# A two-layer MLP on one core: where the sums of the first two passes stand in VectorE's order

## The chip, the cores and the metric

The kernel runs on one core of a Trainium2 chip. The metric is the device time of one execution in microseconds (us), as the median of several executions of the same program. Lower is better.

## The reference

```python
def setup_inputs():
    batch, seq_len, hidden_dim = 8, 1024, 1024
    intermediate_dim = 4 * hidden_dim
    # x (8, 1024, 1024), w1 (1024, 4096), w2 (4096, 1024), all float32

def reference(x, w1, w2):
    h = x @ w1
    h = 0.5 * h * (1 + np.tanh(np.sqrt(2 / np.pi) * (h + 0.044715 * h ** 3)))
    return (h @ w2).astype(np.float32)
```

Two matrix products with a tanh GELU between them: 8192 rows of x, 1024 to 4096 to 1024 columns.

## The kernel before

**Passes.** The 8192 rows are worked in eight passes of 1024 rows (`sb` 0 to 7). A pass is `matmul1` (x times w1, GELU, result g in SBUF) and then a second product (g times w2, rows of the output). The operands are float16, the sums in PSUM and in the `tmp` tiles float32.

**Seven products instead of eight.** Each matrix is cut into 2 x 2 blocks, "11", "12", "21", "22", and the block product is made from seven products of sums of blocks (the Winograd form of Strassen's method). The sums of w are `W_SUM`: sum 5 is 12 - 11, sum 6 is 22 - sum 5, sum 7 is 22 - 12, sum 4 is 21 - sum 6. The sums of x (or g) are `S_SUM`; in `XOps.make` sum 7 is written over block 21. Products 1, 2 and 3 take raw blocks of w. From the third pass on some products are split a second time in the same way; the operands for that ("inner" sums) are made during the first two passes and stored in DRAM.

**The first pass** loads w1 and w2 in float32, casts them and writes the raw float16 blocks to DRAM (`raw_d`, `raw2_d`). **The second pass** (`sb == 1`) reads w1 back in four "quads" of four column chunks (`MadeQuad`): four loads per quad on the SP queue, one per block, then the sums 5, 6, 7, 4 on VectorE, each stored to `w1_d` on the POOL queue, and inner sums (`inner_sums(2)` and `inner_sums(3)`, four small sums each, one store each). Passes three to eight read all of that back ready made and are alike.

**The first m2** is `matmul2_made` with `sb == 0`. Its seven products come in the order 1, 2, 5, 6, 3, 7, 4, each of four row quarters q of 16 matmuls. After a quarter, `post(m, q, bank)` moves the bank out: for products 2, 3 and 7 VectorE adds the bank to a `tmp` tile, for products 1, 5, 6 and 4 ScalarE copies it. Products 6, 7 and 4 go on accumulating in the banks of product 1, so quarter q of product 4 can start only after VectorE has read that bank in `post(7, q)`. After `post`, `run((m, q))` issues the jobs of the table `FILL[0]`: "x5" is sum 5 of the next pass's x, "q5" sum 5 of the first quad of w1, "i2" its inner sums of product 2. The quad's loads are issued at (3, 3); those of the next x are 16 transposing DMAs on the SP queue, issued at (6, 3).

**matmul1 of the second pass** runs over eight pairs j of column chunks. Pair 0 has 12 products of four matmuls, each later pair 14, in the order 1, 1, 4, 4 (of the pair before), 2, 2, 5, 5, 6, 6, 3, 3, 7, 7. VectorE adds the result of product 2 to the tile of product 1 (`add(a[h], banks_b[h])`), then makes `difference(j - 1)`; later it adds product 7 (`add(p5[h], banks_a[h])`) and product 3 (`add(t[h], banks_c[h])`). Product 4 accumulates in the same bank as 1, 6 and 7, so it needs the read of product 7's add. Between these stand the jobs of the pair:

- `ahead(j)`: in an even pair the sums 5 and 6 of the next quad, in an odd pair its sums 7 and 4 and the inner sums 2 and 3;
- `splits`: four sums of a half of a w2 block for the inner level, from `split_in_m1`, for pairs 1 to 4. They work in `gc` tiles, of which there are four: two that a load fills and two for results. The next set's loads wait for the sums that read the tiles before, its sums for the stores (POOL queue, `in_d`) that read the result tiles before.

The first half of the list is issued after `difference`, the rest at the end of the pair. `steady(j)` issues, in four of the pairs, two DMAs each on the POOL queue that cast 256 rows of the x of the third pass to float16 in DRAM (`xb`), each behind a small POOL copy (`pace`) that waits for a GELU.

**Order.** Each engine works through its instructions in order. Matmuls, the VectorE sums with `pin`, copies and GELUs keep the order of the program (`keep_in_program_order`); the other loads and stores are placed by the scheduler.

Of the kernel before, what the change touches and what calls it, by code (L numbers as in the profile page):

```python
# [22 lines left out]
BLOCKS = ("11", "21", "12", "22")  # L23
# [3 lines left out]
SPLIT_IN_M1 = (2, 3)  # L27


def slots(table):  # L30
    return {(int(k[0]), int(k[1])): v.split() for k, v in (row.split(":") for row in table.split(";"))}
# [4 lines left out]
    ;20:g50 w50 w51;21:g51 w52;22:w53 g52;23:g53  # L36
    ;50:w60 w61;51:w62 w63;52:g30 g31;53:g32 g33
    ;60:w70 w71;61:w72 w73;62:w40 w41;63:w42 w43
    ;30:x5;31:x7;32:x6;33:x3
    ;70:q5;71:q6;72:q7;73:q4  # L40
    ;40:i2;41:i3""".replace("\n    ", "")),
    slots("""10:g60 w50;11:g61 w51;12:g62 w52;13:g63 w53
    ;20:g50 p55;21:g51 p56;22:g52 p57;23:g53 p54
    ;50:w60 w61;51:w62 w63;52:g30 g31;53:g32 g33
# [18 lines left out]
def kernel(  # L63
# [7 lines left out]
    nc = tc.nc  # L71
# [33 lines left out]
    raw_d = [dram.tile([P, 4, KH * QW], DT, name=f"raw_d{q}") for q in range(NI // QC)]  # L105
# [4 lines left out]
    def psum():  # L110
        return pp.tile([P, HT], F32, name="ps")

    def temp():
        return tp.tile([P, HT], F32, name="tmp")

    def unit(rows, cols):
        return up.tile([P, rows, cols], DT, name="u")

    def tt(out, in0, in1, op, pin=False):
        i = nc.vector.tensor_tensor(out=out, in0=in0, in1=in1, op=op)  # L120
        if pin:
            tc.keep_in_program_order(i)
# [4 lines left out]
    def flat(t):  # L127
        return t.rearrange("p a b -> p (a b)")
# [31 lines left out]
    class MadeQuad:  # L160


        def __init__(self, q, first, store):
            self.q, self.first, self.store = q, first, store
            self.raw = {b: unit(2 * KH, 2 * P) for b in BLOCKS}
            self.ops = {m: self.raw[b] for m, b in W_TERM.items()}
            if not first:
                for b, t in self.raw.items():
                    nc.sync.dma_start(out=flat(t), in_=raw_d[q][:, BLOCKS.index(b), :])

        def load(self):

# [66 lines left out]
    def stored(d, raw, m):  # L239
        return raw[:, BLOCKS.index(W_TERM[m]), :] if m in W_TERM else d[:, SUMS.index(m), :]  # L240
# [56 lines left out]
    def x_blocks():  # L297
        return {b: unit(KH, HT) for b in ("22", "21", "12", "11")}
# [75 lines left out]
    def x_cast_paced(s, g_chunk, q, xb):  # L374

        mark = nc.gpsimd.tensor_copy(out=pace, in_=g_chunk[:, :2])  # L376
        return x_cast(s, mark, range(q * P, (q + 2) * P, P), xb)

    def x_transpose(xb, dma, blocks=None, which=range(4)):
        blocks = blocks or x_blocks()  # L380
        for b, t in [list(blocks.items())[i] for i in which]:
            a, k = int(b[0]) - 1, int(b[1]) - 1
            for j in range(KH):
                dma(
                    t[:, j, :],
                    xb[a * HT:(a + 1) * HT, (k * KH + j) * P:(k * KH + j + 1) * P],
                    transpose=True,
                )
        return blocks
# [3 lines left out]
    def matmul1(xs, sb, quads, start=None):  # L393
# [69 lines left out]
        def ahead(j):  # L463

            if sb > 1 or j // 2 == NI // QC - 1:
                return ()
            q, second = divmod(j, 2)
            if not second:
                quad = MadeQuad(q + 1, sb == 0, sb == 1)
                quads.append(quad)  # L470
                if sb == 0:
                    quad.load()
                    quads[q].keep_raw()
            quad = quads[q + 1]
            if sb == 0:
                return [lambda m=m: quad.sum(m, pin=True) for m in SUMS] if second else ()
            jobs = [lambda m=m: quad.sum(m, pin=True) for m in ((7, 4) if second else (5, 6))]
            if sb == 1:
                if second:
                    jobs += [lambda m=m: quad.inner_sums(m) for m in INNER_1]  # L480
            return jobs

        def steady(j):

            if 0 < sb < NSB - 1:
                when = (0, 1, 2, 3) if sb > 1 else (0, 1, 5, 6)
                if j in when:
                    nxt["xb"] = x_cast_paced(sb + 1, g["11"][:, 2 * j + 1, :], 2 * when.index(j), nxt.get("xb"))
                if j == 3 and sb > 1:
                    nxt["blocks"] = x_blocks()  # L490
                if j > 3 and sb > 1:
                    x_transpose(nxt["xb"], load_in_order, nxt["blocks"], range(j - 4, j - 3))
            if sb > 1 and j == 5:
                early[7] = gcp.tile([P, NI // 2, HT // 2], GT, name="gc")
                u, v = (inner_block(g["22"], b) for b in ("11", "21"))
                nc.gpsimd.tensor_tensor(out=early[7], in0=u, in1=v, op=SUB)  # L496

        nxt, early = {}, {}
        splits = []
        late = None  # L500
        pending = []
        for j in range(NI // 2):
# [5 lines left out]
            else:  # L508
                source = quads[j // 2]
            jobs = [] if start is not None and j == 0 else list(ahead(j))  # L510
            if sb == 1:
                jobs += splits
                splits = []
            banks_a = [psum(), psum()]
            a = [temp(), temp()]
            for h in range(2):
# [2 lines left out]
            banks_c, p5, t = [], [], [temp(), temp()]  # L519
# [32 lines left out]
            if start is not None and j == 0:  # L552
                start.more()
                quads[0].load_cols(1, 2, 2, nc.gpsimd.tensor_copy)()
                jobs = list(ahead(j))
            half = (len(jobs) + 1) // 2
            for job in jobs[:half]:
                job()
            def six(h):
# [59 lines left out]
                late = (source, cs, banks_a, t)  # L619
            for job in jobs[half:]:  # L620
                job()
            if start is not None and j == 0:
                for m in SUMS:
                    quads[0].sum(m, (2, 2), True)
            if sb == 1 and j < 2 * len(SPLIT_IN_M1):
                m, h = SPLIT_IN_M1[j // 2], j % 2
                splits = split_in_m1(m, h)
            steady(j)
        difference(NI // 2 - 1)
        blocks = nxt.get("blocks")  # L630
# [160 lines left out]
    def split_in_m1(m, h):  # L791

        raw, t = [], {}
        for k in range(2):
            raw.append(gcp.tile([P, 2, HALF], DT, name="gc"))
            q = 2 * k + h
            nc.sync.dma_start(out=flat(raw[k]), in_=stored(w2_d[q], raw2_d[q], m))

        def make(i, n):
            u, op, v = W_SUM[n]  # L800
            if i % 2 == 0:
                t["two"] = gcp.tile([P, 2, HALF], DT, name="gc")
            t[n] = t["two"][:, i % 2]
            in0, in1 = (
                t[b] if isinstance(b, int) else raw[int(b[0]) - 1][:, int(b[1]) - 1] for b in (u, v)
            )
            tt(t[n], in0, in1, op, True)
            nc.gpsimd.dma_start(  # L808
                out=in_d[m][:, i, h * QC:(h + 1) * QC, :].rearrange("p c n -> p (c n)"), in_=t[n]
            )  # L810

        return [lambda i=i, n=n: make(i, n) for i, n in enumerate(SUMS)]

    def inner_block(t, b):
        a, k = int(b[0]) - 1, int(b[1]) - 1
        return t[:, k * NI // 2:(k + 1) * NI // 2, a * HT // 2:(a + 1) * HT // 2]
# [171 lines left out]
    for sb in range(NSB):  # L988
        g, early, nxt = matmul1(xs, sb, quads, first if sb == 0 else None)
        if sb < 2:  # L990
            xs, quads = matmul2_made(sb, g, None if sb else quads[-1].keep_raw, nxt)
            continue
        matmul2(sb, g, early, nxt)
        if nxt is not None:
            xs, quads = nxt, [StoredHalf(0)]
# [30 lines left out]
```

## Time and profile before

| | |
|---|---|
| time, median of 6 runs | 1502.23 us (1497.42 to 1503.43) |
| the profiled execution | 1501.29 us, span 1499.5 us, mean granted TensorE clock 0.998 |
| TensorE busy | 1477.8 us (99% of the span) |
| VectorE busy | 1157.7 us (77%) |
| ScalarE busy | 615.6 us (41%) |
| GpSimd busy | 234.0 us (16%) |
| DMA | 453.70 MB, mean 303 GB/s |
| the pieces of the first two passes | first m2 from 116.9 to 217.0 us, matmul1 of the second pass from 217.0 to 318.6 us, its m2 to about 416 us |

The profile names tiles without buffer numbers: `u` are the tiles of weights and of x, `gc` the staging tiles, `tmp` the float32 tiles, `ps` the PSUM banks, `raw_d` stands for both raw weights in DRAM, `w_d` for the stored sums, `in_d` for the stored inner operands. L399 are the matmuls of matmul1, L900 those of the made m2, L859 those of the inner level; L120 is the helper behind every VectorE sum, L136 the ScalarE copy, L133 a load in order. A bracket behind a row of the timeline is the idle time before it and what ended it. Times in a row are from the span's start.

### The profile page before, as it was taken

What the parts mean: (1) busy time and instruction counts of PE and PEld (TensorE: products, weight loads), DVE (VectorE), ACT (ScalarE), POOL (GpSimd) and SP (SyncE); (2) the same over time, 40 slices, a digit from 0 to 9 for tenths busy, and PEclk for the clock granted to TensorE, in tenths of its full rate; (3) what the DMA queues carried; (4) which work ended last, traced back from release to release, by engine and by line L of the source; (5) the groups of instructions that cost most, each with busy time, mean ns of one, the idle gap of its engine ahead of it and who ended that gap; (6) DMA issues with size and microseconds to landing.
All of it is one profiled execution on the core that took longest, in us unless ns stands there. A gap on an engine that the chain in (4) does not pass through costs nothing.

```text
span 1499.5 us, 26271 instructions
## 1 busy us (share of the span) xinstructions
PE 1477.8 (99%) x9839; PEld 959.5 (64%) x9839; DVE 1157.7 (77%) x1796; ACT 615.6 (41%) x1157; POOL 234.0 (16%) x315
## 2 busy tenths in 40 slices
PE   7999999999999999999999999999999999999998
PEld 3444444444455688557875588755886568855687
DVE  6756548747767799768997799877997779877787
ACT  5665116541056511664126631366214662156510
POOL 3552023202301011010121000110011101101011
PEclk9999999999999999999999999999999999999999
DMA  9999998977898899999999999998999989997896
GB/s 325 340 347 386 256 332 273 395 220 252 316 324 196 307 297 309 342 241 358 295 312 334 220 381 311 302 320 234 360 302 319 292 266 348 295 366 242 296 283 207
DMA packets 242719, 453.70 MB, mean 303 GB/s; under 512 B 80672, under 2 KB 85792, under 8 KB 241696
## 3 DMA queue, kind: packets, MB, share of 16 engines
q1 hardware_dynamic: 215680, 358.69, 71.3%
q0 software_dynamic: 26912, 93.34, 21.1%
q8 instruction: 77, 1.26, 0.3%
q14 instruction: 50, 0.41, 0.1%
HBM read 355.47 MB, written 111.15 MB: 311 GB/s over the span
## 4 chain that ended last, share of the span: by engine, by line
PE 85%; DMA 5%; issue 4%; DVE 3%; SPq 1%; POOL 1%; ACT 1%; POOLq 0%; DVEq 0%; ACTq 0%
PE ps L399 44%; PE ps L859 34%; PE ps L900 7%; DMA u<-in_w_dram 2%; DVE u L120 1%; DVE tmp L120 1%; SPq L133 1%; DMA in_d<-gc 1%; DMA u<-raw_d 1%; DMA u<-in_x_dram 1%; DMA out_dram<-tmp 1%; DMA xb<-in_x_dram 1%; POOL in_d L808 0%; ACT u L136 0%; POOL w_d L214 0%
## 5 line engine op out<-in xcount | busy, mean ns | idle before, releaser
L399 PE MATMUL ps<-u 128*128 128x512 f16 (+1 forms) x4160 | 762.5, 345 | 10.7 <-DVE tmp L120 5.0
L399 PEld LDWEIGHTS <-u 128*128 128x128 f16 x4160 | 407.0, 98 | 363.2 <-issue 19.3
L120 DVE TENSOR_TENSOR tmp<-tmp,ps 128x256 f32<-128x256 f32 (+1 forms) x936 | 453.7, 532 | 238.3 <-PE ps L399 160.9
L136 ACT COPY tmp<-ps 128x512 f32<-128x512 f32 x416 | 234.8, 581 | 303.3 <-PE ps L399 156.9
L412 ACT ACTIVATE g<-tmp 128x512 f16<-128x512 f32 x384 | 241.8, 633 | 174.6 <-DVE tmp L120 174.5
L859 PE MATMUL ps<-u,gc 128*128 128x256 f16 x2688 | 300.4, 273 | 0.0
L859 PEld LDWEIGHTS <-gc 128*128 128x128 f16 x2688 | 262.5, 98 | 31.1
L120 DVE TENSOR_TENSOR u<-u 128x2048 f16<-128x2048 f16 (+3 forms) x296 | 228.3, 810 | 44.2 <-DMA u<-xb 14.8
L859 PE MATMUL ps<-u,g 128*128 128x256 f16 x2016 | 227.9, 273 | 0.0
L136 ACT COPY u<-ps 128x512 f32<-128x512 f32 (+1 forms) x136 | 78.7, 587 | 346.0 <-PE ps L859 341.4
L859 PEld LDWEIGHTS <-g 128*128 128x128 f16 x2016 | 197.2, 98 | 24.1
L650 POOL DMA_DIRECT2D out_dram<-u x70 | 64.0, 988 | 710.2 <-issue 365.8
L120 DVE TENSOR_TENSOR u<-u,ps 128x512 f32<-128x512 f32 x216 | 147.5, 683 | 34.7 <-PE ps L859 28.9
L900 PE MATMUL ps<-u,g 128*128 128x512 f16 x768 | 166.6, 379 | 3.1 <-DVE tmp L120 3.1
L900 PEld LDWEIGHTS <-g 128*128 128x128 f16 x768 | 75.2, 98 | 93.8 <-issue 3.3
L120 DVE TENSOR_TENSOR g<-g,g 128x2048 f16<-128x2048 f16 (+1 forms) x136 | 131.1, 985 | 1.6 <-ACT g L412 1.6
L120 DVE TENSOR_TENSOR gc<-g,gc 128x2048 f16<-128x2048 f16 x84 | 102.3, 1218 | 0.6
L120 DVE TENSOR_TENSOR gc<-g 128x2048 f16<-128x2048 f16 x78 | 94.9, 1217 | 0.0
L412 ACT ACTIVATE g<-ps 128x512 f16<-128x512 f32 x128 | 76.5, 598 | 10.2 <-PE ps L399 6.9
L139 POOL CAST u<-gc 128x1024 f16<-128x1024 f32 x40 | 47.9, 1206 | 39.5 <-DMA gc<-in_w_dram 32.8
L496 POOL TENSOR_TENSOR gc<-g 128x2048 f16<-128x2048 f16 x6 | 24.4, 4064 | 61.6 <-ACT g L412 61.6
L376 POOL COPY pace<-g 128x2 f16<-128x2 f16 x24 | 4.4, 184 | 185.3 <-ACT g L412 185.3
(32 smaller groups left out, 225.9 us busy)
## 6 DMA issues: line engine op xcount, KB each, us to landing
u<-w_d SPq DMA_DIRECT2D x336, 256.0 KB, 6.3
u<-in_d SPq DMA_DIRECT2D x168, 512.0 KB, 6.8
u<-raw_d SPq DMA_DIRECT2D x252, 256.0 KB, 7.1
out_dram<-u POOLq DMA_DIRECT2D x70, 512.0 KB, 9.2
gc<-in_w_dram SPq DMA_DIRECT2D x48, 512.0 KB, 5.8
u<-in_d SPq DMA_DIRECT2D x96, 256.0 KB, 7.5
raw_d<-u SPq DMA_DIRECT2D x32, 512.0 KB, 9.5
u<-raw_d SPq DMA_DIRECT2D x32, 512.0 KB, 9.0
```

The source lines that it names most:

```text
L120: i = nc.vector.tensor_tensor(out=out, in0=in0, in1=in1, op=op)
L133: return tc.keep_in_program_order(nc.sync.dma_start(out=out, in_=in_, **kw))
L136: tc.keep_in_program_order(nc.scalar.copy(out=out, in_=in_))
L139: pool_last[0] = nc.gpsimd.tensor_copy(out=out, in_=in_)
L376: mark = nc.gpsimd.tensor_copy(out=pace, in_=g_chunk[:, :2])
L399: tc.keep_in_program_order(nc.tensor.matmul(bank, lhsT=w, rhs=x, start=first and k == 0, stop=k == n - 1, skip_group_check=not first,))
L412: gelu_last[0] = nc.scalar.activation(out=g[b][:, c, :], in_=src, func=GELU)
L496: nc.gpsimd.tensor_tensor(out=early[7], in0=u, in1=v, op=SUB)
L650: return nc.gpsimd.dma_start(out=rows, in_=src, **kw)
L859: tc.keep_in_program_order(nc.tensor.matmul(bank[:, i * OH // 2:(i + 1) * OH // 2], lhsT=t[:, c, i * P:(i + 1) * P], rhs=self.y[j][:, c, : ...
L900: tc.keep_in_program_order(nc.tensor.matmul(pair(bank), lhsT=a[:, c, :], rhs=chunks(pieces[c // QC])[:, :, c % QC, :], start=(first and c ...
```

## The change

Four edits. In `FILL[0]` the sums of the next x move from product 3 (and those of the quad from product 7) to the end: x5 after (7, 0), x7 after (7, 3), then x6, x3, the quad's sums and the inner sums during product 4. `MadeQuad` loads its blocks in the order 12, 11, 22, 21 instead of 11, 21, 12, 22. In matmul1 of the second pass an even pair issues all its jobs at its end, an odd pair the first three (sum 7, sum 4, inner sums 2) after `difference` and the fourth at its end; the splits always come last in a pair. The casts of x for the third pass are issued in pairs 4, 5, 6, 7 instead of 0, 1, 5, 6.

```diff
@@ FILL[0]
-    ;30:x5;31:x7;32:x6;33:x3
-    ;70:q5;71:q6;72:q7;73:q4
-    ;40:i2;41:i3""".replace("\n    ", "")),
+    ;70:x5;73:x7;40:x6 x3;41:q5 q6;42:q7 q4
+    ;43:i2 i3""".replace("\n    ", "")),
@@ MadeQuad
             if not first:
-                for b, t in self.raw.items():
-                    nc.sync.dma_start(out=flat(t), in_=raw_d[q][:, BLOCKS.index(b), :])
+                for b in ("12", "11", "22", "21"):
+                    nc.sync.dma_start(out=flat(self.raw[b]), in_=raw_d[q][:, BLOCKS.index(b), :])
@@ steady
-                when = (0, 1, 2, 3) if sb > 1 else (0, 1, 5, 6)
+                when = (0, 1, 2, 3) if sb > 1 else (4, 5, 6, 7)
@@ matmul1, the loop over pairs
             jobs = [] if start is not None and j == 0 else list(ahead(j))
-            if sb == 1:
-                jobs += splits
-                splits = []
...
             half = (len(jobs) + 1) // 2
+            if sb == 1:
+                half = 3 if j % 2 else 0
+                jobs += splits
+                splits = []
             for job in jobs[:half]:
                 job()
...
             for job in jobs[half:]:
                 job()
+            if sb == 1 and j < 2 * len(SPLIT_IN_M1):
+                splits = split_in_m1(SPLIT_IN_M1[j // 2], j % 2)
             if start is not None and j == 0:
                 for m in SUMS:
                     quads[0].sum(m, (2, 2), True)
-            if sb == 1 and j < 2 * len(SPLIT_IN_M1):
-                m, h = SPLIT_IN_M1[j // 2], j % 2
-                splits = split_in_m1(m, h)
             steady(j)
```

## The prediction

> **What bounds the kernel now.** I read the page first: TensorE is busy 99% of the span and the chain that ended last is 85% TensorE. So a change can only give back TensorE's idle time, or add to it. Where that idle time lies is told by TensorE's timeline from 110 to 330 us, where first the made m2 (L900) and then matmul1 of the second pass (L399) run.
>
> ```profile
> PE 1477.8 (99%) x9839; PEld 959.5 (64%) x9839; DVE 1157.7 (77%) x1796; ACT 615.6 (41%) x1157; POOL 234.0 (16%) x315
> ```
> ```profile
> 116.87 41.60 PE L900 MATMUL ps<-u,g 128*128 128x512 f16 x192
> ...
> 206.62 10.52 PE L900 MATMUL ps<-u,g 128*128 128x512 f16 x48 [3.05 <-DVE tmp L120]
> 216.97 36.42 PE L399 MATMUL ps<-u 128*128 128x512 f16 x168
> 253.60 24.33 PE L399 MATMUL ps<-u 128*128 128x512 f16 x112 [0.20 <-DVE tmp L120]
> 281.00 37.80 PE L399 MATMUL ps<-u 128*128 128x512 f16 x168 [3.07 <-DVE tmp L120]
> ```
>
> The reader is to see three holes, 3.05, 0.20 and 3.07 us, each ended by a VectorE add out of a bank, and that the last 168 matmuls take 37.80 us where the first 168 take 36.42. In the chain of waits the later passes run on almost without a hole, so what these two passes gain or lose reaches the end undiminished. Why VectorE was late stands in its own timeline (rows of VectorE alone):
>
> ```profile
> 204.74 1.23 DVE L120 TENSOR_TENSOR u<-u 128x2048 f16<-128x2048 f16 x1 [6.10 <-DMA u<-raw_d]
> 205.88 0.68 DVE L120 TENSOR_TENSOR tmp<-tmp,ps 128x512 f32<-128x512 f32 x1
> ...
> 252.25 0.69 DVE L120 TENSOR_TENSOR gc<-gc 128x1024 f16<-128x1024 f16 x1 [3.70 <-DMA gc<-raw_d]
> ...
> 279.66 0.69 DVE L120 TENSOR_TENSOR gc<-gc 128x1024 f16<-128x1024 f16 x1 [3.60 <-DMA in_d<-gc]
> 280.27 2.47 DVE L120 TENSOR_TENSOR tmp<-tmp,ps 128x512 f32<-128x512 f32 x4
> ```
>
> At 204.74 the sum q5 had waited 6.10 us for the quad's load, and the add behind it (`post(7, 1)`) held up product 4. At 252.25 and 279.66 the first split sum stood in the middle of an even pair (2 and 4) and waited for its load, or for the store of the result tile it overwrites; the adds of product 7 queued behind it. The chain says how long that store took: 11.42 us from issue.
>
> **The change part by part.** Nothing is computed anew: the same sums, loads and stores stand in another order. The working is on the clock of the profile before.
>
> *First m2.* Before (7, 1) VectorE now has only x5. It needs the first eight transposes of x; before, the same sum began at 181.78 after waiting for them, and (7, 0) ends at 172.3 + 14.0 (product 3) + 3.5 = 189.8. So x5 no longer waits and the four adds of product 7 follow TensorE by under 1 us. Then come x7, x6, x3, q5, q6, q7, q4 (1.14 us each in a row: seven make 8.0) and eight small sums (0.37 each, 3.0): from 200.7 to 211.7 if the data are there. x7 needs the last transposes, done by 193.35. q5 comes at 204.1 and needs blocks 12 and 11, now the first two loads on SP (192) ahead of the two `gc` loads that preceded them; before, the third of the quad landed at 204.6, behind those two. Product 4 needs no VectorE sum after (7, 3): ScalarE empties its banks. Matmul1 then starts at 200.1 + 13.9 = 214.0 and wants q5 and x5 2.6 us later. On POOL the four stores of quad sums now stand among those of product 4, 0.54 us each, while its tiles are wanted again only in pair 1, over 10 us on. Saved: 3.05 us, and 0.1 us for the 48 matmuls behind the hole (0.219 against 0.217 each). Cost: nothing, covered by 2 us of VectorE slack at 211.7.
>
> *Splits to the end of a pair.* A pair takes 14 x 4 x 0.2168 = 12.1 us. Each set now has a pair between its loads or stores and the next set, where before the sets of pairs 1 and 2, and 3 and 4, were about half a pair apart. The holes of 0.20 and 3.07 us go.
>
> The clock belongs to the last. Windows of 1 us around it:
>
> ```profile
> 278.00:281.00 3.00, 0.00 (x1) 0.90 1.02 396
> 281.00:282.00 1.00, 1.00 (x3) 0.50 1.01 414
> 282.00:283.00 1.00, 1.00 (x4) 0.50 1.05 430
> 283.00:284.00 1.00, 1.00 (x4) 0.59 1.02 418
> 284.00:285.00 1.00, 1.00 (x7) 1.00 1.01 414
> ```
>
> The columns are TensorE's busy time, its granted clock, the DMA share and GB/s. After the hole the clock is halved for some 2.8 us; 37.80 - 36.42 = 1.38 us are lost by it. The Trainium skill (TensorE: Matmul & The Clock Gate, "The HAM clock gate") says that the gate halves the clock after an idle window of about 3.4 us, windows running free. By that rule a hole of 3.07 us costs only itself, and the gain is 3.05 + 0.20 + 3.07 = 6.3. The trace has two such holes: after 206.6 the clock stayed at 1.00, after 281.0 it fell to 0.50. The trace decides: 6.3 + 0.1 + 1.4 = 7.8 us to be had.
>
> *What the new order asks of VectorE.* Pair 2 ends at 251.6; its last add is done at 253.6, then q5, q6 (2.3) and four splits (0.64 each, 2.6) run to 258.5. Pair 3's adds of product 2 could start at 256.8, so they are 1.7 us late; two adds, `difference`, q7, q4 and four small sums (1.2 + 0.6 + 2.3 + 1.5) end at 264.0, the first add of product 7 at 264.6. Product 4 wants it at 263.8 + 1.73 = 265.5. Slack 0.9 us; pair 5 has the same. ScalarE's GELUs of pairs 3 and 5 come as much later, and its copies behind them still beat product 7 by about 1 us. So a VectorE wait at the end of pair 2 or 4 costs TensorE what it exceeds 0.9 us by.
>
> *The wait that could come.* The sets at the ends of pairs 3 and 4 are the critical ones. The second store of the older set is issued near 269.2, and the newer set starts at 280.2. Stores issued there before took:
>
> ```profile
> in_d<-gc POOLq DMA_DIRECT2D x4, 256.0 KB, 11.8
> ```
>
> (DMA issues from 266 to 272 us: number, size, median us to landing.) With the chain's 11.42 us it lands at 280.6: a wait of 0.4, cost nothing. With 12.9, the longest that the in_d rows show, the wait is 1.9 and the cost 1.0. The `gc` load of that set took 9.5 us and is issued near 270.5: about even. I take 0.5 us, near the low end because the row is of the same transfer in the same stretch.
>
> *The casts.* Two pairs' casts leave 226 to 241 us and enter near 275 (pair 4) and 310 (pair 7): per pair 1 MB read and 0.5 MB written. From 264 to 306 the DMA share is already about 1.0 at some 420 GB/s, so pair 4's cast can push others back by at most 1.5 / 0.42 = 3.6 us. The store above is issued 6 us earlier, so I give it none of that; the upper end is 12.9 + 3.6 = 16.5 us to landing, a wait of 5.5, a hole of 4.6 and a half-clock spell of 1.4: 6.0. The lower end is nothing: TensorE has no further idle time to win. Pair 7's cast lands near 320, 60 us before its first sum. On POOL a cast waits for its GELU ahead of w_d stores of q5 and q6, which are not yet made then.
>
> *Loads in the order 12, 11, 22, 21.* In the built order block 21 of the third and fourth quad falls behind the split loads on SP, which wait for VectorE; sum 4 wants it about a pair later. Nothing.
>
> *Sum.* 7.8 - 0.5 = 7.3 us. Profiled execution: 1501.29 - 7.3 = 1494.0. That run is 0.9 us under the median; from the median, 1502.23 - 7.3 = **1494.9 us**.
>
> **The rivals.**
> 1. *Half of it.* The split's wait moves to the end of pair 4 with a cost near that of before (3 us and the clock, 4.4), and only the first m2 gains: 1502.2 - 3.4 = 1498.8 us. For: 11.8 us to landing against 11.0 us of time. Against: the slack of 0.9 us, and fewer casts in flight before 245 us.
> 2. *Slower.* The late casts clog the saturated stretch. The place is the set at the end of pair 4, the price each us that its older stores land later than 11.9 us after issue (11.0 of distance plus 0.9 of slack), plus 1.4 for the clock. With 7.8 regained it decides at 11.9 + 7.8 - 1.4 = 18.3 us; at 22 us the time is 1502.2 + 3.7 = 1505.9. Against: the longest in the trace is 12.9, and 16.5 is the bound above. A wait on w2's first block at the start of the second pass's m2 would need a delay of over 20 us.
> 3. *It does not take.* If q5 is no longer what held product 4 but a late transposed x is, the adds wait on x5 and the first hole stays: 1502.2 - 4.2 = 1498.0. Against: x5's data were there 8 us before.
>
> **How the numbers follow.** Forecast 0.70; half 0.15; first hole stays 0.05; slower 0.08; no difference 0.02. About 0.2% (3.0 us) is what a measurement of this kernel can tell from no change. The forecast and some four fifths of the two half cases are faster by more: 0.86, which I take down to 0.83 for the spread of the runs shown (6 us); the same 0.10, slower 0.07. Range: the full 7.8 with a low median gives 1492.5; up to the half case and 1 us of scatter gives 1500.0.
>
> **What would show it.** Right: TensorE's timeline without holes from 110 to 320 us, the last 168 matmuls of matmul1 as fast as the first, granted clock 1.00 near 280; q5 waiting for nothing or under 1 us; matmul1 starting near 214 and m2 near 311. Wrong: a hole before product 4 of pair 5 with "DVE gc" behind an in_d store or raw_d load; late GELUs holding up product 7; casts landing after 15 us or more.

## The result, and the profile after

The changed kernel takes 1496.37 us (median of 33 runs), the kernel before 1499.82 us (68 runs, those of the table above among them). The ratio is 0.9977, 95% interval 0.9971 to 0.9983: 3.5 us less (2.5 to 4.3), about half of the forecast 7.3. The time itself, 1494.9 forecast and 1496.4 measured, lies nearer than that by luck: the six runs from which the forecast started have a median 2.4 us above that of all 68. The profiled execution took 1499.12 us, span 1497.3 us. TensorE's timeline from 110 to 330 us:

```profile
173.80 41.60 PE L899 MATMUL ps<-u,g 128*128 128x512 f16 x192
215.24 68.37 PE L398 MATMUL ps<-u 128*128 128x512 f16 x316
285.80 30.34 PE L398 MATMUL ps<-u 128*128 128x512 f16 x132 [2.19 <-ACT tmp L135]
315.97 14.19 PE L899 MATMUL ps<-u,g 128*128 128x512 f16 x65
```

(L398 and L899 are the lines L399 and L900 of before, moved up by one.) Products 3, 7 and 4 of the first m2 are one row of 192 matmuls, the first hole is gone. Pairs 0 to 4 of matmul1 have no hole either. One is left, of 2.19 us, 44 matmuls into pair 5, and the 132 matmuls behind it are slow: 0.230 us each against 0.216. VectorE's timeline says what it was waiting for:

```profile
202.23 11.33 DVE L119 TENSOR_TENSOR u<-u 128x2048 f16<-128x2048 f16 x15
...
276.01 2.48 DVE L119 TENSOR_TENSOR u<-u 128x2048 f16<-128x2048 f16 x2
280.06 1.42 DVE L119 TENSOR_TENSOR gc<-gc 128x1024 f16<-128x1024 f16 x2 [1.57 <-DMA in_d<-gc]
282.72 1.29 DVE L119 TENSOR_TENSOR gc<-gc 128x1024 f16<-128x1024 f16 x2 [1.24 <-DMA in_d<-gc]
283.93 1.28 DVE L119 TENSOR_TENSOR tmp<-tmp,ps 128x512 f32<-128x512 f32 x2
```

The first row is all the moved sums of the first m2 in one run, x7 to the inner sums, without a wait. The next rows are the end of pair 4: q5 and q6, then the last split set, which waits twice, once for each of its two result tiles, for the stores of the set before. The adds of product 2 of pair 5 come only at 283.93. The chain of waits goes through the second of these waits:

```profile
269.06 13.56 DMA in_d<-gc
...
284.01 0.61 DVE tmp L119
...
285.18 0.57 ACT tmp L135
...
285.80 30.34 PE ps L398 x132
```

The store took 13.56 us from issue. Behind it come a VectorE add, a GELU and then a ScalarE copy; TensorE waited for that copy. By the order of pair 5 the 44 matmuls before the hole are eleven products, so it stands before the second half of product 3, which goes on accumulating in the second bank of product 5: the copy is the one that empties this bank. The issues from 262 to 272 us (number, size, median us to landing) show that the store was no stray one:

```profile
in_d<-gc POOLq DMA_DIRECT2D x4, 256.0 KB, 12.5
gc<-raw_d SPq DMA_DIRECT2D x2, 512.0 KB, 9.5
```

And the clock (TensorE busy, PEld, DVE, ACT, POOL busy, then granted clock, DMA share, GB/s):

```profile
285.00:286.00 1.00, 0.20 (x1) 0.10 (x1) 1.00 (x3) 1.00 (x3) 0.00 (x0) 1.00 1.03 422
286.00:287.00 1.00, 1.00 (x6) 0.48 (x5) 1.00 (x2) 1.00 (x3) 0.00 (x0) 1.00 0.99 406
287.00:288.00 1.00, 1.00 (x4) 0.30 (x2) 1.00 (x2) 0.24 (x1) 0.81 (x1) 0.50 1.04 426
288.00:290.00 2.00, 2.00 (x6) 0.76 (x5) 1.97 (x6) 0.00 (x0) 1.65 (x4) 0.50 1.03 422
290.00:295.00 5.00, 5.00 (x23) 2.21 (x22) 3.71 (x9) 4.31 (x8) 1.59 (x3) 0.96 1.05 383
```

The clock falls to half only 1.2 us after the matmuls have begun again, for about 3.4 us. In a kernel below with a hole there but no such spell, the same 132 matmuls take 28.73 us; so the spell costs 1.6 us and the hole with it 3.8.

A profile shows one execution, and executions of one kernel differ: the first m2 starts between 116.9 and 118.6 us, and where its sums of w2 come late, products 5 and 6 have holes that sum to between 0 and 3.5 us in the profiles below, in code that no kernel changes. The profiled execution of the changed kernel is 2.75 us above its median. So I read the parts of a profile by their own length, and the times by their intervals. Each ratio below is to runs of the kernel before taken alongside, with medians of 1499.0 to 1500.2 us. The length of matmul1 of the second pass, from its first matmul to that of m2, is 101.7 us before and 100.7 after; without holes it is 96.7.

### The profile page after: what moved, and what is told of

Read it like the earlier page. It is cut to its first block, busy times and chain, and to the rows that moved or that the text cites. A ratio compares the mean times of both kernels' runs of the same rounds, so it can differ in the third digit from the quotient of the medians.

```text
span 1497.3 us, 26273 instructions
## 1 busy us (share of the span) xinstructions
PE 1480.4 (99%) x9839; PEld 961.7 (64%) x9839; DVE 1154.2 (77%) x1796; ACT 615.7 (41%) x1157; POOL 233.7 (16%) x315
## 4 chain that ended last, share of the span: by engine, by line
PE 83%; issue 7%; DMA 5%; DVE 2%; POOL 2%; ACT 0%; SPq 0%; POOLq 0%; DVEq 0%; ACTq 0%
PE ps L398 43%; PE ps L858 34%; PE ps L899 6%; DMA u<-w_d 2%; DMA in_d<-gc 1%; DVE tmp L119 1%; DVE u L119 1%; DMA u<-in_w_dram 1%; DMA xb<-in_x_dram 1%; DMA u<-raw_d 1%; DMA in_d<-u 1%; POOL out_dram L637 0%; POOL w_d L213 0%; POOL in_d L807 0%; DMA u<-in_d 0%
## 5 line engine op out<-in xcount | busy, mean ns | idle before, releaser
L398 PE MATMUL ps<-u 128*128 128x512 f16 (+1 forms) x4160 | 763.2, 346 | 10.2 <-DVE u L119 4.7
L398 PEld LDWEIGHTS <-u 128*128 128x128 f16 x4160 | 407.3, 98 | 363.2 <-issue 18.0
L119 DVE TENSOR_TENSOR u<-u 128x2048 f16<-128x2048 f16 (+3 forms) x296 | 224.0, 795 | 18.7 <-ACT u L135 8.1
L899 PE MATMUL ps<-u,g 128*128 128x512 f16 x768 | 166.4, 379 | 0.0
L899 PEld LDWEIGHTS <-g 128*128 128x128 f16 x768 | 75.2, 98 | 90.6
```

What stands on the lines that cost most here:

```text
L398: tc.keep_in_program_order(nc.tensor.matmul(bank, lhsT=w, rhs=x, start=first and k == 0, stop=k == n - 1, skip_group_check=not first,))
L899: tc.keep_in_program_order(nc.tensor.matmul(pair(bank), lhsT=a[:, c, :], rhs=chunks(pieces[c // QC])[:, :, c % QC, :], start=(first and c ...
```

## The experiments

My theory after the result: the hole of pair 5 is VectorE's two waits for the stores of the set at the end of pair 3. Two explanations of why those stores are slow were set against each other: the cast that the change puts into pair 4 (A), or a stretch that is full whatever the casts do (B).

**The first m2 alone.** The kernel before with the new row of `FILL[0]` and the new load order.

```diff
-    ;30:x5;31:x7;32:x6;33:x3
-    ;70:q5;71:q6;72:q7;73:q4
-    ;40:i2;41:i3
+    ;70:x5;73:x7;40:x6 x3;41:q5 q6;42:q7 q4
+    ;43:i2 i3
...
-                for b, t in self.raw.items():
+                for b in ("12", "11", "22", "21"):
...
```

> The first m2's part alone: the new FILL[0] row and the load order 12, 11, 22, 21; matmul1 of the second pass as before. My theory: the hole before product 4 (3.05 us) goes and nothing else does; the holes in matmul1 (0.20 and 3.07 us, with the clock 1.4) stay: 3.2 us faster than before, ratio 0.998. Rival (the later quad sums push a wait into matmul1): matmul1's part grows and the gain is under 1.5 us.

Measured: 1498.18 us, ratio to before 0.9984 (0.9974 to 0.9994), 2.4 us less (0.9 to 3.9). TensorE's timeline:

```profile
172.61 41.60 PE L899 MATMUL ps<-u,g 128*128 128x512 f16 x192
214.05 36.42 PE L398 MATMUL ps<-u 128*128 128x512 f16 x168
250.65 24.33 PE L398 MATMUL ps<-u 128*128 128x512 f16 x112 [0.17 <-DVE tmp L119]
277.80 36.42 PE L398 MATMUL ps<-u 128*128 128x512 f16 x168 [2.82 <-DVE tmp L119]
```

The first hole goes, the two in matmul1 stay where they were. This time the hole of 2.82 us was followed by no half-clock spell: the last 168 matmuls take 36.42 us, as the first 168 do.

**The late jobs alone.** The changed kernel with the old table, the old load order and the old casts.

```diff
-    ;70:x5;73:x7;40:x6 x3;41:q5 q6;42:q7 q4
-    ;43:i2 i3
+    ;30:x5;31:x7;32:x6;33:x3
+    ;70:q5;71:q6;72:q7;73:q4
+    ;40:i2;41:i3
...
-                for b in ("12", "11", "22", "21"):
+                for b, t in self.raw.items():
...
-                when = (0, 1, 2, 3) if sb > 1 else (4, 5, 6, 7)
+                when = (0, 1, 2, 3) if sb > 1 else (0, 1, 5, 6)
```

> The late jobs alone: quad sums and splits late in a pair, but FILL[0], the load order and the casts of x (pairs 0, 1, 5, 6) as before. Theory A (pair 4's cast delays the stores that the last set waits for): with no cast in pair 4 the store lands in about 11.4 us, VectorE waits under 1 us, no hole at pair 5, and the gain is the whole 4.4 to 4.7 us of matmul1, ratio 0.997. Rival B (the stretch is saturated anyway, and the stores of a set need 13 us whatever the casts do): the hole at pair 5 stays at 2 us or more with its half-clock spell, and the gain is 1 us or less, ratio 0.9995.

Measured: 1501.46 us, ratio 1.0015 (1.0002 to 1.0028): slower than before, if by little. Neither A nor B said so. TensorE's hole at pair 5 was 3.66 us with a half-clock spell, and VectorE's timeline names another wait:

```profile
164.51 13.07 PE L900 MATMUL ps<-u,gc 128*128 128x512 f16 x52 [2.54 <-DVE u L120]
177.42 41.65 PE L900 MATMUL ps<-u,g 128*128 128x512 f16 x192
...
291.42 30.34 PE L399 MATMUL ps<-u 128*128 128x512 f16 x132 [3.66 <-ACT tmp L136]
```
```profile
285.88 1.23 DVE L120 TENSOR_TENSOR u<-u 128x2048 f16<-128x2048 f16 x1 [4.48 <-DMA u<-raw_d]
```

This is q6 of the fourth quad, and what it lacks is block 22. So the load order had to be tried by itself. The first two rows show something else: though the table is the old one, products 3, 7 and 4 of the first m2 are one row of 192 here. TensorE had lost 2.7 us in holes at products 5 and 6, the last of them that of 2.54, and a half-clock spell on top, and reached product 4 after its adds. The hole of 3.05 us is thus not in every execution of the old table.

**The old load order.** The changed kernel with that one edit undone.

```diff
-                for b in ("12", "11", "22", "21"):
-                    nc.sync.dma_start(out=flat(self.raw[b]), in_=raw_d[q][:, BLOCKS.index(b), :])
+                for b, t in self.raw.items():
+                    nc.sync.dma_start(out=flat(t), in_=raw_d[q][:, BLOCKS.index(b), :])
```

> The changed kernel with the quad's blocks loaded in the old order 11, 21, 12, 22. My prediction gave the order nothing. If that holds, the profile and the time are those of the changed kernel, ratio to before 0.9977. The run with late jobs, old table, old casts and old order speaks against it: there sum 6 of the fourth quad waited 4.48 us for block 22, the fourth load. If the order is the cause, a wait of 3 us or more for a raw_d load appears at the end of pair 4 here too, with a hole of 2.5 us or more, and the time is 1 to 3 us above the changed kernel, ratio 0.9985 to 0.9995.

Measured: 1502.05 us, ratio to before 1.0016 (1.0006 to 1.0026), against 0.9977 for the changed kernel. TensorE:

```profile
288.84 30.31 PE L398 MATMUL ps<-u 128*128 128x512 f16 x132 [5.36 <-ACT tmp L135]
```

The SP queue and VectorE of the same kernel:

```profile
268.42 0.98 SPq L796 DMA_DIRECT2D gc<-raw_d  x2
269.50 0.79 SPq L168 DMA_DIRECT2D u<-raw_d  x1
```
```profile
275.89 1.22 DVE L119 TENSOR_TENSOR u<-u 128x2048 f16<-128x2048 f16 x1
283.30 1.23 DVE L119 TENSOR_TENSOR u<-u 128x2048 f16<-128x2048 f16 x1 [6.19 <-DMA u<-raw_d]
```

With late splits the fourth load of a quad stands behind the two split loads on SP, which wait for VectorE's sums at the end of pair 3. In the old order that fourth load is block 22: issued at 269.5, wanted by q6 at 277.1, and there when q6 starts at 283.3. In the new order it is block 21, wanted only by sum 4 in the next pair. The order is what makes the late jobs pay. In the first m2 it changes nothing that shows: with the old order, too, the fifteen moved sums run there in one row of 11.33 us.

**The old casts.** The changed kernel with the casts in pairs 0, 1, 5, 6.

```diff
-                when = (0, 1, 2, 3) if sb > 1 else (4, 5, 6, 7)
+                when = (0, 1, 2, 3) if sb > 1 else (0, 1, 5, 6)
```

> The changed kernel with the casts of x put back to pairs 0, 1, 5, 6. Theory A: the wait of the last set shrinks below 1 us, the hole of 2.19 us and the half-clock spell (1.7 us) go: 3.9 us faster than the changed kernel, ratio to before 0.995. Rival B: the hole stays, ratio 0.9975 as for the changed kernel, or worse, as the early casts delay the first sets' loads.

Measured: 1495.80 us, ratio 0.9973 (0.9962 to 0.9984), not to be told from the changed kernel. VectorE and TensorE:

```profile
284.00 1.42 DVE L119 TENSOR_TENSOR gc<-gc 128x1024 f16<-128x1024 f16 x2 [0.61 <-DMA in_d<-gc]
286.66 1.29 DVE L119 TENSOR_TENSOR gc<-gc 128x1024 f16<-128x1024 f16 x2 [1.25 <-DMA in_d<-gc]
```
```profile
289.74 28.73 PE L398 MATMUL ps<-u 128*128 128x512 f16 x132 [1.24 <-ACT tmp L135]
```

The waits sum to 1.86 us against 2.81, and the hole is 1.24 against 2.19: 0.95 less in both. The stores landed in 11.6 us (median) against 12.5. So A is right for about 1 us of the wait and wrong for the rest. No half-clock spell follows the shorter hole, so by the two profiles matmul1 is 2.6 us shorter than in the changed kernel; the times do not show that gain, nor do those of the next run, where it is as large.

**The loads of w2 held back.** A transfer of 512 bytes in front of them on SP reads a GELU result of pair 5.

```diff
+        if sb:
+            load_in_order(hold_d, g["11"][:, 10, :2])
         bring("11", pool_copy, False)
```

> The changed kernel with one more SP transfer, of 512 bytes, in front of the loads of w2 for the second pass's m2: it reads a GELU result of pair 5, so that the sixteen w2 loads (512 KB each), seven of which are issued between 269.7 and 283.1 us in the changed kernel, are held until pair 5's GELU near 286 us. Theory A (the early w2 loads and the cast of pair 4 share the DMA engines with the stores of pair 3's split set): without the w2 loads those stores land in 10 to 11 us instead of 12.5 to 13.6, VectorE waits under 1 us for them, and the hole at pair 5 is under 0.5 us: 3 us faster than the changed kernel, ratio to before 0.9955. Rival B (the stores are slow because of what was issued before them: the sums of quad three, the loads of quad four and the split loads): landing stays above 12 us and the hole at 1.5 us or more, ratio 0.9975. m2 starts near 311 us and its first w2 block would land near 295, so the hold costs nothing there, unless the later blocks land after their product.

Measured: 1495.94 us, ratio 0.9978 (0.9966 to 0.9990). The w2 loads began at 283.4. TensorE, and the stores issued from 266 to 270 us:

```profile
283.52 28.73 PE L399 MATMUL ps<-u 128*128 128x512 f16 x132 [1.19 <-ACT tmp L136]
```
```profile
in_d<-gc POOLq DMA_DIRECT2D x4, 256.0 KB, 12.1
```

Again a fall of about 1 us in the hole, and stores that still take 12.1 us. VectorE's two waits were 1.14 and 0.66 us. B is nearer: most of the 12 us comes from neither of the two streams that I took away, one at a time. Which of the others it is (stores of the quad's sums, loads of the fourth quad, the split loads) was not separated.

**Three sets on other pairs.** Sets at the ends of pairs 1, 3, 5, 6 instead of 1, 2, 3, 4.

```diff
+SPLIT_AFTER = (0, 2, 4, 5)
...
-            if sb == 1 and j < 2 * len(SPLIT_IN_M1):
-                splits = split_in_m1(SPLIT_IN_M1[j // 2], j % 2)
+            if sb == 1 and j in SPLIT_AFTER:
+                n = SPLIT_AFTER.index(j)
+                splits = split_in_m1(SPLIT_IN_M1[n // 2], n % 2)
```

> The changed kernel with the four split sets at the ends of pairs 1, 3, 5, 6 instead of 1, 2, 3, 4, so that no set stands behind the quad sums of an even pair and the third set has two pairs' time for the stores before it; the casts stay in pairs 4 to 7. Both theories: the wait at the end of pair 4 goes with its hole and clock, so 3.9 us faster than the changed kernel, ratio 0.995. If a wait remains at pair 6 (stores of the set of pair 5, 12 us before, with casts in flight), VectorE has no jobs behind it there and 2 us or more of slack: no hole under theory A or B. If a third cause (TensorE waiting for ScalarE's copies in any case) were behind the hole of 2.19 us, it would stay.

Measured: 1495.17 us, ratio 0.9974 (0.9964 to 0.9984). The hole at pair 5 went, matmul1 took 97.5 us with one hole of 0.64, but in this profile, of the slowest of its ten runs (1501.08 us), the gain was spent elsewhere. The SP queue, and TensorE later:

```profile
266.60 25.44 SPq L798 DMA_DIRECT2D gc<-raw_d  x4
292.12 26.50 SPq L133 DMA_DIRECT2D u<-raw_d  x16
```
```profile
406.93 3.61 PE L901 MATMUL ps<-u,g 128*128 128x512 f16 x16 [1.63 <-DVE tmp L120]
...
423.31 3.34 PE L399 MATMUL ps<-u 128*128 128x512 f16 x16 [0.90 <-DMA u<-raw_d]
427.97 81.00 PE L399 MATMUL ps<-u 128*128 128x256 f16 x468 [1.31 <-DMA u<-in_d]
```

The last split loads wait for pair 5's sums and stand before w2's loads on SP, so these start at 292.1 instead of 269.7. A sum of w2 then waits 4.91 us for one of them, and holes appear at the end of m2 and the start of the third pass, which the changed kernel does not have. I read these as its consequence; how the delay travels there was not followed.

**Only the last set moved**, from the end of pair 4 to that of pair 5: the edit above with `SPLIT_AFTER = (0, 1, 2, 4)`.

> The changed kernel with only the last split set moved, from the end of pair 4 to the end of pair 5; the other sets stay at pairs 1, 2, 3. The stores it waits for then have two pairs, some 24 us, and the split loads stay ahead of the loads of w2 in SP's order. Theory: no wait for a store, no hole at pair 5 nor pair 6, matmul1 of the second pass in 97.5 us or less; ratio to before 0.995. Rival (the sums at the end of pair 5 push a hole into pair 6): a hole of 1 us or more at pair 6, ratio 0.9970 or more.

Measured: 1493.87 us, ratio 0.9959 (0.9945 to 0.9973), 6.1 us less than before (4.0 to 8.2). This is the lowest median of all, though its interval overlaps those of the next two kernels. TensorE:

```profile
214.21 96.86 PE L399 MATMUL ps<-u 128*128 128x512 f16 x448
310.90 41.60 PE L901 MATMUL ps<-u,g 128*128 128x512 f16 x192
```

All 448 matmuls of matmul1 in one row.

**Result tiles of their own.** The changed kernel with the sets where they are, but their result tiles from the larger pool.

```diff
-                t["two"] = gcp.tile([P, 2, HALF], DT, name="gc")
+                t["two"] = up.tile([P, 2, HALF], DT, name="u")
```

> The changed kernel, but the result tiles of the split sums (two) come from the pool of 26 u tiles instead of the four gc tiles, so that a set no longer waits for the stores of the set before it. Theory (the hole of pair 5 is VectorE's two waits for in_d stores, 1.57 and 1.24 us, minus some 0.6 us of slack): no such waits, no hole at pair 5, matmul1 of the second pass in 97.5 us or less against 100.7, and 3.5 to 3.9 us less than the changed kernel, ratio to before 0.995. Rival (the stretch is saturated, so VectorE then waits for the gc load of the same set or for a quad's load instead): a wait of 1 us or more by another name and a hole of 1 us or more at pair 5. The eight u tiles taken may also make loads of w2 later, at a cost at the start of the next m2.

Measured: 1494.84 us, ratio 0.9963 (0.9950 to 0.9977). No VectorE wait for a DMA in the whole of matmul1, and the same single row:

```profile
215.24 96.86 PE L398 MATMUL ps<-u 128*128 128x512 f16 x448
```

This and the run above take the same wait away by different means, and with it the hole: that the stores of the set before were the cause of the hole is shown. What the hole costs is less in the times than in the profile: against 0.9977 for the changed kernel the two ratios are 2.7 and 2.1 us less, not the 3.5 to 3.9 expected, and all these intervals overlap. So the cause rests on the profiles, and the price of the hole in the times is known only roughly.

**The last set moved, old casts.**

> As the kernel with the last split set at the end of pair 5, and the casts of x back in pairs 0, 1, 5, 6. If the late casts only lengthen the stores that the last set waits for, they cost nothing once that set has two pairs: the same time as that kernel within 1 us. If the early casts hurt (they share the queue with the first quad's loads), a hole appears in pairs 1 to 3 and it is 1 us or more slower; if the late casts hurt elsewhere (the start of the second pass's m2), it is faster.

Measured: 1494.47 us, ratio 0.9968 (0.9957 to 0.9979); matmul1 in 96.7 us without a hole. Its interval overlaps that of the kernel with late casts: once nothing waits for the stores, where the casts stand can't be told by the time. Its gain over the changed kernel is 1.3 us.

## Why the prediction was right in part, point by point

- **First m2: right.** 3.15 us were forecast; the hole is gone, products 3, 7 and 4 with their holes take 41.4 us where they took 44.7, and the edit alone gives 2.4 (0.9 to 3.9). x5 waited for nothing, the moved sums ran in one row from 202.2 to 213.6 (11.3 us, worked out as 11.0).
- **Splits to the end of a pair: right for the first three sets.** The hole of 0.20 us is gone, and no set up to pair 3 waits.
- **The wait that could come: the mis-sized term.** I put 0.5 us for the set at the end of pair 4; in the profile it cost 3.8, in three parts. The landing was taken as 11.42 us, the one store on the chain of before; it was 12.5 in the median and 13.56 for the last, and VectorE waited 1.57 us for the first result tile, of which 0.95 came through the slack. I counted one wait only; the second tile waits again for later stores, 1.24 us more. And the half-clock spell was put at the upper end only, while a hole of 2.19 us already brought it, 1.6 us.
- **The 7.8 us to be had: right for one profile, too much for the times.** The three kernels without the hole of pair 5 gain 4.8, 5.5 and 6.1 us on before, and are by their medians only 1.3 to 2.7 us faster than the changed kernel, with intervals that overlap its own. Two of the summed terms stood in the one profile of before and are absent from others: the kernel with the new first m2 has a hole of 2.82 us without the half-clock spell, and the one with late jobs alone has no first hole. How often each is absent was not counted, so how the miss of 3.8 us divides between this sum and the wait stays open.
- **The slack: nearly right, by another route.** I worked out 0.9 us to product 4 by way of VectorE's add of product 7. The waits minus the holes are 2.81 - 2.19, 1.86 - 1.24 and 1.80 - 1.19 us in three kernels: 0.62, 0.62 and 0.61. What TensorE meets first is ScalarE's copy of product 5's second bank, late behind a GELU that waits for the add of product 2. I had given ScalarE's copies about 1 us, but up to product 7; the second half of product 3, just before it, already waits for one.
- **The casts: "none of that" was about 1 us too little**, by one profile with the late casts and one without: the stores issued before the cast of pair 4 landed later with it, 12.5 against 11.6 us.
- **The load order: "nothing" was true of block 21 and missed what the order is for.** Undone, it costs 0.39 points of ratio (0.9977 to 1.0016), since block 22 then takes the place behind the split loads. I had costed the edit as made and not asked what the other edits would cost without it.
- **The rival "half of it"** is what happened, by its mechanism and place: 7.8 - 3.8 = 4.0 us by the profiles, 3.4 as written there. That the median's 3.5 meets the 3.4 so closely is in part luck, as the times bear out neither the 7.8 nor the whole cost of the hole. The slower rival's point of decision, 18.3 us to landing, was not reached; but the same stretch does turn the change into a loss by another load when the order is undone.

## What to carry to other kernels

When a sum is moved later to get out of a wait, ask what its result tile and its operands wait for at the new place: a store that took 11 us in a full stretch may take 13, and each rotating tile has a wait of its own. A load queue in order is part of such a move: whatever comes to stand behind a load that waits for a compute engine should be what is wanted last. And where a stretch has all DMA engines busy, giving the waiting work one more period can be worth more than making one of its neighbours go away: here the first took the hole away, the second left more than 1 us of it.

## What the runs showed that I had not expected

- **The clock after a hole.** In the first m2 and the second pass of all these kernels, holes of 1.97, 2.19, 2.54, 3.07, 3.66 and 5.36 us were followed by a spell at 0.50; holes of 2.82 and 3.05 us were not, nor any of 1.78 or less. The same 52 matmuls of product 6 of the first m2, with the old casts and then with the last set moved and the old casts:

```profile
165.79 13.07 PE L899 MATMUL ps<-u,gc 128*128 128x512 f16 x52 [1.97 <-DVE u L119]
```
```profile
163.75 11.38 PE L901 MATMUL ps<-u,gc 128*128 128x512 f16 x52 [1.78 <-DVE u L120]
```

In the 2.19 us case the spell began 1.2 us after the matmuls had resumed. So neither the idle window of about 3.4 us, which the prediction quotes from the Trainium skill (TensorE: Matmul & The Clock Gate, "The HAM clock gate"), nor the length of the hole alone tells: between about 2 and 3 us a hole costs itself, or 1.4 to 1.7 us more.

- **Streams taken away give little in a full stretch.** Moving the cast or the seven w2 loads away took the stores from 12.5 us to 11.6 and 12.1.
